# The output projection of a transformer layer as seven products of half-size blocks, on one NeuronCore of Trainium2

## The chip, the cores and the metric

The kernel runs on one core of a Trainium2 chip. The core has five engines that run side by side: TensorE (PE in the profile; its weight loads are shown as PEld), VectorE (DVE), ScalarE (ACT), GpSimd (POOL) and SyncE (SP), which here only starts transfers. SBUF is the on-chip memory of 128 partitions, PSUM the eight banks into which TensorE writes (one bank holds 128 x 512 float32). The metric is the device time of one execution in microseconds; lower is better.

## The reference

One decoder layer over 1024 tokens of width 1024, in float32 (DEPTH = 1, so alpha = 2^(1/4)):

```python
h = x @ w_in                      # columns: pool | q | k | v | forget gate
pool = pool_mixer(h[pool])        # 4 groups of 128 channels, trailing means over 2, 4, 8, 16 tokens minus
                                  # the token, then a 128 x 128 linear map and a scale per channel
attn = forgetting_attention(q, k, v, f)      # 8 heads of 64, causal, logit bias from cumulated log gates
x = layer_norm(alpha * x + concat(pool, attn) @ w_out)
x = layer_norm(alpha * x + square(relu(x @ w_mlp1)) @ w_mlp2)
```

`w_out` is 1024 x 1024: the output projection is a product of (tokens x mixture channels) with (mixture channels x output channels).

## The kernel before

**Precision.** Every float32 operand of a large product is split into a high part (rounded to the matmul's own format, `fp32r`) by ScalarE and a low part (the rest) by VectorE; `split` (line 70) makes both. A product then takes three matmuls, high x high, high x low and low x high (`three`, line 80).

**Buffers.** SBUF tiles come from five tags with a fixed number of buffers (line 48): S 3, U 2, B 14, Q 10, A 9. A B buffer holds 8 KB per partition, the others about 4. A tile gets a buffer when an earlier tile of its tag has been used for the last time; until then whatever writes it waits. PSUM banks are tags too: s 3, pt 2, pv 1, mm 2.

**Order.** The program is written out in Python, one instruction after the other; a planner, which knows the buffers and a cost for each operation, makes from it one fixed order per engine at build time. Within an engine, instructions run in that order, each behind its semaphores. `tc.issue_after(i)` puts the instructions traced in its block behind instruction i on i's engine.

**Stages.** (1) Values and gates of all tokens (lines 165 to 210); as this runs, blocks 3 to 7 of `w_out` are loaded, split and written to DRAM as high and low parts (`wo_dram`, lines 190 to 210). (2) The pooling groups 3, 2 and 1 (`pool_group`, line 264, 48 matmuls of 512 columns each) and the first key and query projection (`qk_proj(0)`). Each group's linear map (`pool_linear`) is 6 matmuls; its result goes to `mix_dram`. (3) Four pairs of heads, each in 8 units of 256 queries (loop at line 680): `att_probs` makes the probabilities, `att_values` transposes them and multiplies with V. Between the steps of a unit `fillstep` (line 669) takes pieces of other matmul work from a generator, at a rate that spreads it over the pair: in pairs 0 to 2 the next pair's projection, in the last pair `last_fill` (line 485): the projection of pooling group 0 in two halves, its linear map, the loads of the output weights and the output rows 0 and 1. Each output row is 2 halves x 8 blocks x 3 matmuls (`out_proj`, line 576), the mixture's transposed blocks being the weights (`mixes`) and `w_out`'s rows the moving operand. (4) After the pairs, rows 2 to 7 (loop at line 916): load x, the matmuls, then `normed` (line 592), which adds alpha x + product and norms the row on VectorE, and `x1_transposed` (line 736), which transposes a normed row with TensorE and makes the blocks that the MLP's products need. (5) The MLP, whose two products are already made as seven half-size products each (Winograd's form: A11, A12, A22, S1 to S4 on one side, B11, B21, B22, T1 to T4 on the other). Its first products, `first.p1` to `third.p2`, use A11 and A12 only (rows 0 to 3); `first.p6` is the first that needs S2, into which all rows go.

The attention results are stored unscaled in `mix_dram` and the reciprocal row sums in `rin_dram`; `attention_part` (line 548) loads both and multiplies.

## Time and profile before

| | us |
|---|---|
| median of 3 runs | 1033.78 |
| lowest, highest | 1032.7, 1034.51 |
| the profiled execution, its own time | 1033.61 |
| its span in the profile | 1031.8 |
| TensorE busy | 1015.8 |
| VectorE busy | 755.0 |
| ScalarE busy | 513.6 |
| GpSimd busy | 157.3 |

The profile is one execution. A matmul's recorded duration is longer than the time at which the next one can follow, since matmuls are pipelined; what a matmul costs is read from the distance of starts or from the chain that ended last, where it is shown as length of a run of matmuls. "Busy" leaves out waits and the instructions that only issue transfers. L12 is line 12 of the kernel.

### The profile page before, as it was taken

How to read it: one execution, taken by the hardware profiler on the slowest of the kernel's cores; microseconds unless marked ns; L12 is line 12 of the kernel's file. 1: busy time of each engine (PE TensorE's matmuls, PEld its weight loads, DVE VectorE, ACT ScalarE, POOL GpSimd, SP SyncE). 2: the span in 40 equal slices, each digit the busy share in tenths (PEclk: the TensorE clock that was granted, in tenths of full speed). 3: DMA queues.
4: the chain of work that ended last, by engine and by line, in shares of the span. 5: the costliest groups of instructions: out<-in, count | busy, mean ns of one | idle time of the engine just before them, and what ended most of it. 6: DMA issues, size and time to landing. Idle time of an engine off the chain costs nothing.

```text
span 1031.8 us, 14130 instructions
## 1 busy us (share of the span) xinstructions
PE 1015.8 (98%) x4976; PEld 845.6 (82%) x4976; DVE 755.0 (73%) x1303; ACT 513.6 (50%) x825; POOL 157.3 (15%) x269
## 2 busy tenths in 40 slices
PE   9999999999999999999999999999999999999996
PEld 9988888888787888788888888888888888888884
DVE  6576777777767897989878778888866575565547
ACT  5423666666655332677766666668521121121152
POOL 0200112111110032112122121120100000000057
PEclk9999999999999999999999999999999999999998
DMA  9703311111483632239666566665999888878753
GB/s 358 283 23 107 100 52 46 37 30 62 144 286 131 197 141 103 81 132 371 250 264 258 229 258 244 239 253 195 356 300 300 284 284 265 280 239 272 236 181 122
DMA packets 113463, 206.17 MB, mean 200 GB/s; under 512 B 9640, under 2 KB 77672, under 8 KB 113392
## 3 DMA queue, kind: packets, MB, share of 16 engines
q1 hardware_dynamic: 94240, 136.97, 40.3%
q0 software_dynamic: 18720, 67.64, 17.0%
q8 instruction: 39, 0.64, 0.3%
q10 hardware_dynamic: 432, 0.66, 0.2%
q14 instruction: 32, 0.26, 0.1%
HBM read 132.29 MB, written 72.94 MB: 199 GB/s over the span
## 4 chain that ended last, share of the span: by engine, by line
PE 57%; DVE 2%; issue 0%; ACT 0%; DVEq 0%
PE s L1109 17%; PE s L769 11%; PE pv L1109 9%; PE mm L769 7%; PE pt L769 7%; PE pv L769 4%; PE pt L1109 2%; PE mm L1109 2%; DVE B L71 0%; DVE bns L613 0%; DVE A L638 0%; DVE pt L635 0%; DVE pt L1126 0%; DVE A L843 0%; DVE pv L1126 0%
## 5 line engine op out<-in xcount | busy, mean ns | idle before, releaser
L71 ACT CAST B<-S 128x1024 fp32r<-128x1024 f32 (+1 forms) x78 | 67.6, 880 | 162.1 <-DMA S<-in_w_dram 95.2
L769 PE MATMUL s<-B,Q 128*128 128x512 f32 x492 | 116.4, 389 | 0.2 <-ACT B L71 0.2
L769 PEld LDWEIGHTS s<-B,Q 128*128 128x128 f32 x492 | 92.3, 188 | 19.8 <-ACT B L71 0.7
L71 DVE TENSOR_TENSOR B<-S,B 128x1024 fp32r<-128x1024 f32 (+1 forms) x78 | 78.1, 1008 | 36.4 <-ACT B L71 36.3
L1109 PE MATMUL s<-B,Q 128*128 128x512 f32 x402 | 98.5, 390 | 0.0
L1109 PEld LDWEIGHTS s<-B,Q 128*128 128x128 f32 x402 | 75.5, 188 | 16.4
L71 ACT CAST Q<-S 128x1024 fp32r<-128x1024 f32 (+2 forms) x54 | 55.6, 1030 | 55.5 <-PE s L769 17.0
L894 POOL DMA_DIRECT2D hid_dram<-A x90 | 48.1, 538 | 218.2 <-ACT A L891 171.5
L1109 PE MATMUL s<-B,A 128*128 128x512 f32 x321 | 80.0, 394 | 0.0
L769 PE MATMUL pt<-B,Q 128*128 128x512 f32 x312 | 74.5, 389 | 0.0
L71 DVE TENSOR_TENSOR Q<-S,Q 128x1024 fp32r<-128x1024 f32 (+2 forms) x54 | 65.5, 1212 | 12.3 <-ACT Q L71 12.2
L1109 PEld LDWEIGHTS s<-B,A 128*128 128x128 f32 x321 | 60.4, 188 | 13.8
L769 PE MATMUL mm<-B,Q 128*128 128x512 f32 x300 | 71.6, 389 | 0.0
L769 PEld LDWEIGHTS pt<-B,Q 128*128 128x128 f32 x312 | 58.5, 188 | 12.1
L769 PEld LDWEIGHTS mm<-B,Q 128*128 128x128 f32 x300 | 56.3, 188 | 11.7
L423 PEld LDWEIGHTS pv<-A,B 128*128 128x128 f32 x320 | 51.1, 188 | 17.6 <-ACT A L403 7.0
L382 ACT ACTIVATE A<-A,nm 128x1024 f32<-128x1024 f32 (+7 forms) x64 | 49.7, 777 | 31.5 <-DVE nm L380 31.0
L423 PE MATMUL pv<-A,B 128*128 128x256 f32 x320 | 61.2, 293 | 3.2 <-DVE A L404 1.5
L404 DVE TENSOR_TENSOR A<-pt,A 128x512 fp32r<-128x512 f32 (+1 forms) x80 | 49.9, 633 | 16.7 <-ACT A L403 16.0
L892 DVE TENSOR_TENSOR A<-A,A 128x1024 f32<-128x1024 f32 x45 | 53.6, 1219 | 0.0
L366 POOL TENSOR_TENSOR A<-A,maskb 128x128 f32<-128x128 f32 x48 | 23.6, 494 | 194.4 <-DVE nm L380 132.0
L403 ACT CAST A<-pt 128x512 fp32r<-128x512 f32 (+1 forms) x80 | 41.4, 542 | 21.9 <-PE pt L402 21.2
(432 smaller groups left out, 2320.0 us busy)
## 6 DMA issues: line engine op xcount, KB each, us to landing
hid_dram<-A POOLq DMA_DIRECT2D x105, 512.0 KB, 3.9
S<-in_w_dram SPq DMA_DIRECT2D x62, 512.0 KB
Q<-hid_dram SPq DMA_DIRECT2D x98, 256.0 KB
A<-hid_dram SPq DMA_DIRECT2D x82, 256.0 KB
S<-in_wuqk_dram SPq DMA_DIRECT2D x12, 512.0 KB
wo_dram<-Q POOLq DMA_DIRECT2D x10, 512.0 KB, 4.5
B<-wo_dram SPq DMA_DIRECT2D x10, 512.0 KB
Q<-hid_dram SPq DMA_DIRECT2D x39, 128.0 KB
```

The source lines that it names most:

```text
L71: return nc.scalar.copy(hi, src).ins, nc.vector.tensor_tensor(lo, src, hi.bitcast(F32), ALU.subtract).ins
L366: nc.gpsimd.tensor_tensor(nb[:, qs], nb[:, qs], maskb, ALU.add)
L382: nc.scalar.activation(pt[:, :nk], pt[:, :nk], AF.Exp, bias=nm, scale=-1.0, accum_out=rsum[h][:, i : i + 1])
L403: nc.scalar.copy(tt[:, 0, ev], tp[:, ev])
L404: fill["sub"] = nc.vector.tensor_tensor(tt[:, 1, ev], tp[:, ev], tt[:, 0, ev].bitcast(F32), ALU.subtract).ins
L423: nc.tensor.matmul(ov, V[j][:, h].rearrange("p s d -> p (s d)"), tt[:, s, a:b], start=(j == 0 and s == 0), stop=(j == 2 * m + 1 and s == 1),)
L769: nc.tensor.matmul(dst, b[x][:, k], A[a][y][:, k], start=first and k == 0 and i == 0, stop=k == H - 1 and i == 2, skip_group_check=not first,)
L892: nc.vector.tensor_tensor(x, x, hi.bitcast(F32), ALU.subtract)
L894: nc.gpsimd.dma_start(hid_dram[self.u, :, i, AT[name] : AT[name] + 2 * CH], part.rearrange("p q n t -> p (q n t)"))
L1109: nc.tensor.matmul(dst, h[:, p_], w[q_], start=first and u == self.us[0] and j == 0, stop=u == self.us[-1] and j == 2, skip_group_check=no ...
```

## The change

The output product Y = M W is taken as 2 x 2 blocks of 512: M's columns are the pooled half (4 blocks of 128 channels) and the attention half, its rows the first and last 512 tokens; W's rows and columns are split likewise. With M11 = pooled part of the later tokens (the order of the token halves is turned so that the pooled halves come first), Winograd's form needs seven products of (512 x 512) x (512 x 512) in place of eight: A11 x B11, S3 x T3, S2 x T2, S1 x T1, A22 x T4, A12 x B21, S4 x B22.

- **Weights.** All of `w_out` is loaded in front, in four pairs of blocks (k and k + 4). `output_sums` forms T1 to T4 with four subtractions on GpSimd per k, `split_output_weights` makes high and low parts of B11; B21, B22; T1, T2 and T3, T4 (ScalarE, and VectorE or GpSimd), and all go to `wo_dram` (7 versions x 2 parts). Two of the four k are done between the value products, two between the pooling groups.
- **Pooling groups.** All four (3, 2, 1, 0) run in front of the pairs as `pool_group`, and all their linear maps too. `late_group`, `late_linear` and the old `last_fill` go.
- **Fill.** In the last quarter of pair 2's fill (`third_fill`), B11 is loaded and A11 and the pooled differences are made (`pooled_differences`). The last pair's fill is three of the seven products, A11 x B11, S3 x T3 and S2 x T2, 12 bank results, each copied to SBUF (`kept`) by ScalarE and, for the third product, added into the other two on GpSimd. Each attention product is queued behind the last fill piece (before: for the first 8 pieces only).
- **Attention blocks.** `first_part` and `later_part` load, scale and combine attention results with the pooled ones to S2, A22, S1, A12 and S4, in steps after the units of the last pair, and for the last 256 tokens after the pairs.
- **Rows.** After the pairs, four products are left. A first loop over r makes S1 x T1 and A22 x T4 and finishes rows 0 to 3; a second makes A12 x B21 and S4 x B22 and finishes rows 4 to 7. Rows 0 to 5 are normed with ScalarE and GpSimd (`on_pool`), 6 and 7 on VectorE. Three rows (5, 6, 7) are transposed among the first MLP products (before: row 7 alone).

```diff
+    WEIGHTS = ("B11", "B21", "B22", "T1", "T2", "T3", "T4")
+    wo_dram = dr.tile([len(WEIGHTS), 2, P, NG, CH], F32, name="wo_dram")
...
+    def output_sums(k):
+        (b1, b2), sub = raw[k], nc.gpsimd.tensor_tensor
+        t12, t34 = slot("Q", [2, CH], F32), slot("Q", [2, CH], F32)
+        sub(t12[:, 0], b1[:, 1], b1[:, 0], ALU.subtract)
+        sub(t12[:, 1], b2[:, 1], t12[:, 0], ALU.subtract)
+        sub(t34[:, 0], b2[:, 1], b1[:, 1], ALU.subtract)
+        sub(t34[:, 1], b2[:, 0], t12[:, 1], ALU.subtract)
+        raw[k] = ((0, b1[:, 0:1]), (1, b2), (3, t12), (5, t34))
+
+    def split_output_weights(k, i, tag, eng):
+        n, src = raw[k][i]
+        w = src.shape[1]
+        hi = slot(tag, [w, CH])
+        nc.scalar.copy(hi, src)
+        eng.tensor_tensor(src, src, hi.bitcast(F32), ALU.subtract)
+        for j, part in enumerate((hi.bitcast(F32), src)):
+            nc.gpsimd.dma_start(wo_dram[n : n + w, j, :, k].rearrange("n p c -> p n c"), part)
...
+            n = 2 * (t - 4) + half
+            if n % 4 == 0:
+                output_sums(n // 4)
+            split_output_weights(n // 4, n % 4, "S", nc.vector)
...
-    for g in EARLY:
+    for n, g in enumerate(POOLS):
+        if n in (1, 2):
+            load_output_weights(n + 1)
         run(pool_group(g, None, "A"))
-        if g == EARLY[0]:
+        if n == 0:
             gate_sum(neglog)
+        else:
+            if n > 1:
+                pool_linear(POOLS[n - 2], "A")
+            if n < 3:
+                output_sums(n + 1)
+                for i in range(4):
+                    split_output_weights(n + 1, i, "A", nc.vector if i < 2 else nc.gpsimd)
...
-    pool_linear(EARLY[0], "A")
+    pool_linear(POOLS[2], "A")
     run(g0)
+    pool_linear(POOLS[3], "A")
...
+    def pooled_differences(c):
+        new, old = pooled_part(2 + c), pooled_part(c)
         if c == 0:
+            kept["S"] = slot("B", F32B, F32)
+        put("A11", c, new, "B")
+        nc.gpsimd.tensor_tensor(kept["S"][:, c], new, old, ALU.subtract)
...
+    def block_product(dst, name, weight, r):
+        (hi, lo), w = mixes[name, r // 2], wo[weight]
+        ts_ = slice(r % 2 * P, (r % 2 + 1) * P)
+        for k in range(NG):
+            yield three(dst, (hi[:, k, ts_], lo[:, k, ts_]), (w[0][:, k], w[1][:, k]), k == 0, k == NG - 1)
+
+    def third_fill():
+        for n, _ in enumerate(qk_proj(NPAIR - 1, "mm")):
+            yield
+            if n == 23:
+                output_weights("B11")
+                for c in range(2):
+                    pooled_differences(c)
+
+    def last_fill():
+        output_weights("T3")
+        for c in range(2):
+            put("S3", c, kept["S"][:, c], "Q")
+        for n, (name, weight) in enumerate((("A11", "B11"), ("S3", "T3"), ("S2", "T2"))):
+            kept[n] = slot("B", [NT // 2, CH], F32)
+            for r in range(NT // 2):
+                dst = bank("mm")
+                yield from block_product(dst, name, weight, r)
+                nc.scalar.copy(kept[n][:, r], dst)
+                if n == 2:
+                    nc.gpsimd.tensor_tensor(kept[2][:, r], kept[2][:, r], kept[0][:, r], ALU.add)
+                    nc.gpsimd.tensor_tensor(kept[1][:, r], kept[1][:, r], kept[2][:, r], ALU.add)
+                if n == 0 and r == NT // 2 - 1:
+                    output_weights("T2")
...
+    def normed(t, xt):
         nm = Norm(xt, *gb, x1_dram[t])
-        for i, c in enumerate(nm.cols):
-            nc.vector.scalar_tensor_tensor(xt[:, c], xt[:, c], ALPHA, yp[i], ALU.mult, ALU.add)
-            nm.stats(i)
-        nm.on_vector(nc.gpsimd)
+        if t < NT - 2:
+            nm.on_pool()
+        else:
+            for i in range(2):
+                nm.stats(i)
+            nm.on_vector(nc.gpsimd)
...
+    load_rows()
+    output_weights("T1", "T4")
...
+    for r in range(4):
+        a, b = row(r), row(4 + r)
+        a0, a1, b0, b1_ = (y_[:, c] for y_ in (a, b) for c in both)
+        for half in (a0, a1):
+            stt(half, half, ALPHA, kept[1][:, r], ALU.mult, ALU.add)
+        p5, p4 = bank(), bank()
+        run(block_product(p5, "S1", "T1", r))
+        into(a1, a1, p5, ALU.add)
+        stt(b1_, b1_, ALPHA, p5, ALU.mult, ALU.add)
+        run(block_product(p4, "A22", "T4", r))
+        into(a0, a0, p4, ALU.add)
+        nc.gpsimd.tensor_tensor(b1_, b1_, kept[2][:, r], ALU.add)
+        stt(b0, b0, ALPHA, pre[:, r], ALU.mult, ALU.add)
+        normed(r, a)
+        if r == 0:
+            step(3, 1)
+        if r == 1:
+            step(3, 2)
+            output_weights("B21", "B22")
+        if r == 3:
+            x1_transposed(*done.pop(0))
+    for r in range(4):
...
+        b0, b1_ = (x[4 + r][:, c] for c in both)
+        p2, p3 = bank(), bank()
+        run(block_product(p2, "A12", "B21", r))
+        into(b0, b0, p2, ALU.add)
+        run(block_product(p3, "S4", "B22", r))
+        into(b1_, b1_, p3, ALU.add)
+        normed(4 + r, x[4 + r])
+        x1_transposed(*done.pop(0))
...
     first.p1()
     first.p2()
     first.split_t2()
+    x1_transposed(*done.pop(0), ("mm", "pv"))
     second.p1()
-
-    block("S2", lambda j: R1[j][:, 0], 3)
+    x1_transposed(*done.pop(0), ("mm", "pv"))
     second.sums()
     second.split_t2()
+    block("S2", lambda j: R1[j][:, 0], 3)
     x1_transposed(*done.pop(0))
```

More of the change, by code (lines that the diff above doesn't have):

```diff
@@ new lines, in trunk, with output_weights, put @@
+    mixes, wo, done, gb = {}, {}, [], []
+    F32B = [2, NG, 256]
+    def output_weights(*names):
+        for name in names:
+            wo[name] = slot("B", [NG, CH]), slot("B", [NG, CH])
+            for i, part in enumerate(wo[name]):
+                nc.sync.dma_start(part.bitcast(F32), wo_dram[WEIGHTS.index(name), i])
+    def put(name, c, src, tag):
+        if tag == "B":
+            both = slot("B", F32B)
+            mixes[name, c] = hi, lo = both[:, 0], both[:, 1]
+        else:
+            mixes[name, c] = hi, lo = slot(tag, [NG, 256]), slot(tag, [NG, 256])
+        split(hi, lo, src)
@@ new lines, in pooled_part, with attention_part @@
+    def pooled_part(m):
+        mf = slot("S", [NG, 256], F32)
+        nc.sync.dma_start(mf, mix_dram[m, :, 0:NG, :])
+        return mf
+    def attention_part(m):
+        mf, rb = slot("S", [NPAIR, 256], F32), slot("S", [NPAIR, 256], F32)
+        nc.sync.dma_start(mf, mix_dram[m, :, NG : 2 * NG, :])
+        for e in range(2):
+            rows = rin_dram[e::2, m * 256 : (m + 1) * 256].rearrange("(o p) t -> o p t", o=1)
+            nc.sync.dma_start(rb[e * HD : (e + 1) * HD], rows.to_broadcast([HD, NPAIR, 256]))
+        return mf, rb
@@ L584, in trunk, with two, later_part, one @@
-    gb = []
+                nc.gpsimd.tensor_tensor(kept["S"][:, c], mf, kept["S"][:, c], ALU.subtract)
+                put("S2", c, kept["S"][:, c], "Q")
+        def two():
+            with tc.issue_after(fill["sub"]):
+                nc.gpsimd.tensor_tensor(old, mf, old, ALU.add)
+                put("A22", c, mf, "B")
+                put("S1", c, old, "B")
+        return one, two
+    def later_part(c):
+        mf, rb = attention_part(2 + c)
+        def one():
+            with tc.issue_after(fill["sub"]):
+                nc.vector.tensor_tensor(mf, mf, rb, ALU.mult)
+                nc.gpsimd.tensor_tensor(kept["S"][:, c], mf, kept["S"][:, c], ALU.subtract)
+                put("A12", c, mf, "Q")
+        def two():
+            with tc.issue_after(fill["sub"]):
+                put("S4", c, kept["S"][:, c], "Q")
+        return one, two
@@ L673, in fillstep @@
             piece = next(fill["gen"], None)
-            if piece and fill["pieces"] < 8:
-                fill["piece"], fill["pieces"] = piece, fill["pieces"] + 1
+            if piece:
+                fill["piece"] = piece
     order = [(p, e, m) for p in range(NPAIR - 1) for e in range(2) for m in (3, 2, 1, 0)]
@@ L679, in trunk, with step @@
     pend = None
+    parts = {}
+    def step(m, i):
+        if m < 0:
+            return
+        if i == 0:
+            parts[m] = first_part(m) if m < 2 else later_part(m - 2)
+        else:
+            parts[m][i - 1]()
     for n, unit in enumerate(order):
@@ new lines, in trunk, with row @@
+    output_weights("T1", "T4")
+    pre, x, both = kept[0], [None] * NT, (slice(0, CH), slice(CH, D))
+    stt, into = nc.vector.scalar_tensor_tensor, nc.vector.tensor_tensor
+    rr[0] = 0
+    def row(t):
+        x[t] = slot("A", [D], F32)
+        nc.sync.dma_start(x[t], xn[t])
+        return x[t]
+    for r in range(4):
[19 more added lines that the diff above has]
+            x1_transposed(*done.pop(0))
@@ new lines, in trunk @@
+    for r in range(4):
+        if r == 3:
+            for un in units[:2]:
+                un.load_f()
+                un.split_f("Q" if un.u else "B")
+                if un.u == 0:
+                    un.load_g()
+                    un.sums(nc.gpsimd)
+        b0, b1_ = (x[4 + r][:, c] for c in both)
[6 more added lines that the diff above has]
+        x1_transposed(*done.pop(0))
```

185 lines of the change are left out of this document (28 added, 157 removed).

## The prediction

> **What bounds the kernel now.** I read the page's busy times first, then busy time by stage, then the chain that ended last.
>
> ```profile
> span 1031.8 us, 14130 instructions
> PE 1015.8 (98%) x4976; PEld 845.6 (82%) x4976; DVE 755.0 (73%) x1303; ACT 513.6 (50%) x825; POOL 157.3 (15%) x269
> ```
>
> TensorE is busy 98% of the span. That is an average, so the next view gives the busy time of each engine stage by stage (columns: the stretch, its length, then PE, weight loads, DVE, ACT, POOL, each with its count, granted clock, DMA share, GB/s).
>
> ```profile
> 50.00:109.00 59.00, 59.00 (x273) 48.92 (x272) 38.62 (x78) 17.39 (x28) 0.76 (x1) 1.00 0.19 66
> 109.00:267.00 158.00, 156.16 (x909) 130.22 (x908) 116.42 (x288) 101.81 (x220) 30.08 (x74) 1.00 0.18 56
> 267.00:338.00 71.00, 68.15 (x385) 55.08 (x385) 51.79 (x125) 42.23 (x90) 7.48 (x15) 1.00 0.58 194
> 338.00:406.00 68.00, 68.00 (x327) 56.78 (x326) 56.58 (x97) 18.85 (x33) 16.32 (x18) 1.00 0.46 155
> 406.00:424.70 18.70, 18.46 (x90) 14.82 (x88) 18.31 (x32) 12.07 (x21) 2.93 (x4) 1.00 0.17 61
> ```
>
> The stretches are the pooling groups with the first projection, pairs 0 to 2, the last pair, the output projection of rows 2 to 7, and the first MLP products up to the first that needs row 7. PE idles only 2.85 us in the last pair, 1.84 in the pairs before, and nowhere in the output projection. So matmuls taken away are worth their full time if nothing new stalls PE. The fifth row warns: there VectorE is busy 18.31 of 18.70 us. The chain says the same (start, length, work):
>
> ```profile
> 415.57 1.20 DVE B L71 x2
> ...
> 423.38 0.61 DVE Q L758
> 424.00 0.02 issue
> 424.02 0.63 ACT B L71
> 424.65 0.04 issue
> 424.69 8.50 PE s L769 x36
> 433.19 2.72 PE pt L769 x12
> ```
>
> Up to 424.69 the chain runs through VectorE, making block S2 of the MLP's operand out of row 7; from there it is PE. PE loses only 0.24 us there, but VectorE has nothing to give. The last row gives the price of a matmul of 512 columns: 2.72 / 12 = 0.2267 us.
>
> **The change part by part.** **Matmuls.** The output product had 8 row tiles x 2 halves x 8 blocks x 3 = 384 matmuls; seven products of 4 row tiles x 4 blocks x 3 make 336. Ahead of the pairs 54 are added (48 of group 0's projection, 6 of its linear map; +12.2 us), the fill of the last pair goes from 150 to 144 (-1.4), and what follows the pairs from 288 to 192 (-21.8). Together 48 fewer: **-10.9 us**. Transposes, attention and MLP products are the same.
>
> **Last pair.** Group 0's projection, its two linear maps and the output rows 0 and 1 leave the fill, and with them the waits of their loads. Of the 2.85 us that PE idles there I count 1.0 as gone; bounds -2.8 (all gone) and 0, since new waits (A11 and S2 from DRAM) can take their place: **-1.0 us**.
>
> **Where the tail begins.** Today all output weights are in SBUF before the pairs end. In the change the fourth product needs T1 (hi and lo, 1 MB each) in two of the 14 buffers of tag B. Counting buffers through the last pair: V holds 4, T2 2, the kept products 3, A22 and S1 2 each, the difference S 1: 14, all taken. T1 gets buffers only when T2's last fill matmul or V's first tiles are done, and the gain and shift rows of the norm are in front of it. The fill ends two steps before the last attention product, since each attention product is now queued behind its fill piece. The nearest rows for these two steps are the last ones of today's last pair (PE, in order of time):
>
> ```profile
> 333.48 0.49 PE L402 MATMUL pt<-ident,A 128*128 128x128 f32 x3
> 333.72 0.73 PE L423 MATMUL pv<-A,B 128*128 128x256 f32 x4
> 334.54 0.50 PE L423 MATMUL pv<-A,B 128*128 128x256 f32 x2
> 335.80 0.40 PE L423 MATMUL pv<-A,B 128*128 128x256 f32 x2
> ```
>
> They last 2.7 us. For the load, the DMA view (KB, us from issue to landing) and one stretch of today's weight loads:
>
> ```profile
> x_dram<-A POOLq DMA_DIRECT2D x12, 256.0 KB, 2.6
> out_dram<-Q POOLq DMA_DIRECT2D x4, 512.0 KB, 3.2
> 298.00:300.00 2.00, 2.00 (x16) 1.82 (x15) 2.00 (x7) 1.29 (x2) 0.00 (x0) 1.00 1.04 408
> ```
>
> 256 KB more cost 0.6 us, so 2.0 is fixed, and 2 MB land 2.0 + 8 x 0.6 = 6.8 us after issue. 6.8 - 2.7 = 4.1 us of idle PE; the rows of gain and shift (1 MB, 2.5 us at 408 GB/s) start some 1.5 us earlier and push a little. I take **+4.5 us**, bounds 2 (V's first tile serves T1 early) and 7 (all of the rows' 2.5 us ahead of it). While it waits, VectorE and POOL work off what is ready.
>
> **The tail's other engines.** Rows 0 to 5 are now normed by ScalarE and POOL, and POOL adds more. What an add costs, and what POOL and VectorE do to each other (POOL's four sums of the first MLP unit, the norm passes and splits of VectorE with POOL active and without, the POOL norm's groups at the kernel's end, transposes):
>
> ```profile
> 365.19 1.29 POOL L817 TENSOR_TENSOR S<-S,S 128x512 f32<-128x512 f32 x1 [7.11 <-DVE B L71]
> 366.56 1.62 POOL L818 TENSOR_TENSOR U<-S,S 128x512 f32<-128x512 f32 x1
> 368.14 1.74 POOL L820 TENSOR_TENSOR S<-S 128x512 f32<-128x512 f32 x1
> 369.84 2.28 POOL L819 TENSOR_TENSOR S<-U,S 128x512 f32<-128x512 f32 x1
> 363.89 1.21 DVE L71 TENSOR_TENSOR B<-S,B 128x1024 fp32r<-128x1024 f32 x1
> 365.33 3.40 DVE L635 SCALAR_TENSOR_TENSOR A<-A,mv,B 128x512 f32<-128x512 f32 x2
> 368.73 2.23 DVE L71 TENSOR_TENSOR Q<-S,Q 128x1024 fp32r<-128x1024 f32 x1
> 376.52 1.40 DVE L635 SCALAR_TENSOR_TENSOR A<-A,mv,B 128x512 f32<-128x512 f32 x2
> L652 POOL TENSOR_TENSOR Q<-Q,S 128x1024 f32<-128x1024 f32 x4 | 9.6, 2411 | 265.4 <-ACT Q L651 265.4
> L646 ACT ACTIVATE U<-Q,rt 128x1024 bf16<-128x1024 f32 x4 | 4.6, 1149 | 0.1
> L651 ACT ACTIVATE Q<-Q,rt 128x1024 f32<-128x1024 f32 x4 | 5.0, 1240 | 3.0 <-DVE rt L650 3.0
> 405.88 0.60 PE L742 MATMUL pv<-ident,A 128*128 128x128 f32 x4
> 406.31 0.60 PE L742 MATMUL mm<-ident,A 128*128 128x128 f32 x4
> 406.67 2.98 PE L769 MATMUL s<-B,B 128*128 128x512 f32 x12
> ```
>
> The two scale passes took 3.40 us against 1.40, the split 2.23 against 1.21: VectorE lost 3.0 us, and POOL's four adds 6.93 - 4 x 1.29 = 1.8, while they overlapped. Lost together 4.8 of 5.2 us: an operation of VectorE that reads two operands from SBUF runs in turn with a POOL add, not beside it. So I sum both as one resource, from the pairs' end to the first product that needs row 7. POOL: 4 adds of 512 columns for the lower rows, 6 norms of 2 x 2.41, unit 0's four sums, some 3 adds of transposed rows: 11 x 1.29 + 28.9 = 43 us. VectorE with two SBUF operands: 12 scaled adds of a half row (0.7 each, half an L635 pair), four passes of 1.21 on the last operands, 8 scale passes of rows 6 and 7, two unit splits, some 15 half passes for transposed rows, T2, S2 and unit sums: 35 x 0.7 + 6 x 1.21 = 32. Together 75 us. PE in that stretch: 192 x 0.2267 = 43.5, eight rows of transposes at 0.79 (405.88 to 406.67), six products of 2.72: 66 us. 9 us too much, of which the 4.5 us at the front and the head start of adds on products already made absorb the larger part. I take **+2.7 us**, bounds 0 (unit sums and splits done early, as POOL's rows at 365 show today, 40 us ahead of their use) and 9.
>
> **Pooling groups and weights.** Group 0 joins the stage at 50 to 109, with the weights' sums and splits. VectorE's 38.62 us there grow by group 0 (4 passes of 1.21) and six splits for two of the four k (3.8 us); POOL adds per k four sums and two splits, 4 x 1.29 + 2 x 2.41 = 10, 20 us for two k, all in turn with VectorE in the worst case: 67 us, in a stage that grows to 59 + 12.2 = 71. It fits, with little left; PE has eight banks and the next group's weights ahead of it. The weight parts go out by POOL's DMA queue and are 14.7 MB, written and read, against 5.2; at 408 GB/s the added writes are 23 us of a queue that this stage uses at 0.19. I take **+1.0 us**, bounds 0 and 5 (a group's weights late by one 1.21 pass and one POOL split, at two group changes).
>
> Sum: -10.9 - 1.0 + 4.5 + 2.7 + 1.0 = -3.7 us. The profiled execution took 1033.61 us (1.81 outside its span), 0.17 below the median of 1033.78, so 1029.9 there and **1030** for the median.
>
> **The rivals.** *All is hidden:* loads and adds find room, and only the matmuls and part of the last pair's idle time count, -10.9 - 0.5: 1022. For it: PE runs through equally crowded stages without a gap today. Against it: the count of B buffers, which leaves T1 no place earlier.
>
> *DMA eats it, no net change:* behind T1 queue T4 (2 MB), row vectors (1), eight rows of x (4), the last attention part (1), B21 and B22 (4): 14 MB with T1, 35 us at 408 GB/s. PE wants B22 about 4.5 + 21.8 + 2.7 + 0.8 = 30 us after the pairs, 32.5 after the fill. Late by 2.5 to 3, if x rows don't come in before: 1033. Against it: T4 may wait behind row 1's T1 product, and four to eight buffers of tag A fall free as attention ends, so x can come early.
>
> *Slower, the tail set by POOL and VectorE in turn:* the first norm reaches POOL only after 5.4 us of PE plus about 5 us of ScalarE and VectorE (two passes of 1.1, one of 1.24, small ones). From there some 66 of the 75 us remain, ending at 10.9 + 66 = 77 against PE's 66: +11 in place of +2.7, in total +4.6: 1038. It decides for a loss once the tail costs more than 10.9 + 1.0 - 4.5 - 1.0 = 6.4 us. For it: the 4.8 of 5.2 us above, and VectorE's 18.31 of 18.70. Against it: adds that read PSUM need not share.
> [...]
>
> **How the numbers follow.** Forecast 0.32, all hidden 0.13, DMA 0.22, POOL and VectorE in turn 0.33. 0.2%, 2.1 us, is about what a measurement of this kernel tells from no change: faster 0.45 (the first two), same 0.22, slower 0.33. The forecast's own range is 1026 to 1031.5. All bounds at their best give 1022, at their worst 1044; I keep 1023 to 1040 for 8 in 10.
>
> **What would show it.** PE matmuls fall from 4976 to 4928. Right for the front: the first product with T1 waits 2 to 7 us for a DMA from the weights in DRAM, after the last attention product. Right for the tail: POOL nearly full between the pairs' end and the first product with S2, VectorE's two-operand passes stretched, PE waiting a few us for a transposed row or S2. Right for the groups: PE without gaps of over 1 us before pair 0. Wrong if T1 is there in time, if waits for B21 or B22 show, or if a product in the last pair's fill holds up attention by several us.

## The result, and the profile after

The changed kernel takes 1098.41 us (median of four runs, 1095.05 to 1099.71) against 1033.49 of the kernel before on the same chip: a ratio of 1.0623, interval 1.0596 to 1.0649. It is 6% slower, where 1030 was forecast and 1040 was the top of the range. The profiled execution took 1097.66, its span is 64.1 us longer than before. The page of the changed kernel (busy times and, in 40 slices, the granted TensorE clock in tenths):

```profile
span 1095.9 us, 14175 instructions
...
PE 1030.9 (94%) x4928; PEld 851.6 (78%) x4928; DVE 788.8 (72%) x1293; ACT 548.6 (50%) x876; POOL 267.0 (24%) x330
...
PEclk9989989999999887989999999999999999999998
```

The 48 matmuls are gone, as forecast (4928 against 4976), and yet TensorE is busy 15.1 us longer and idle 65.0 us in place of 16.0. With 10.9 us fewer to do, that is 26 us of slower matmuls and 49 us of new idle time: 26 + 49 - 10.9 = 64. The slices show the first part. In the kernel before every slice was at 0.9 of full speed or more (mean 0.997), and now the mean is 0.967; behind the wait for group 3's weights it is 0.50 (57.00 to 61.00), the half clock of the text below:

```profile
PEclk9999999999999999999999999999999999999998
```

TensorE's instructions of the changed kernel in order of time say where it was lost (start, length, work, and in brackets the idle time ahead and what ended it):

```profile
137.71 0.77 PE L401 MATMUL s<-Q,Q 128*128 128x512 f32 x1 [4.59 <-DVE Q L369]
...
374.94 0.97 PE L449 MATMUL pv<-A,B 128*128 128x256 f32 x6 [0.23 <-DVE A L430]
...
415.07 1.11 PE L758 MATMUL s<-ident,A 128*128 128x128 f32 x4 [7.09 <-POOL A L652]
...
484.88 8.49 PE L785 MATMUL s<-B,Q 128*128 128x512 f32 x36
```

And the same place in the kernel before, beside the last attention product (335.80) and the first MLP product with S2 (424.69) shown in the prediction:

```profile
108.31 1.07 PE L375 MATMUL s<-Q,Q 128*128 128x512 f32 x4
```

The first attention score, the end of the last attention product and the first MLP product with S2, which needs every normed row, cut the span in four. (The row at 415.07 is the first transpose of a normed row.) "Expected" is the kernel before with the matmuls added or removed by the prediction's count and nothing else:

| stretch | before | expected | after | lost |
|---|---|---|---|---|
| to the first score | 108.3 | 120.5 | 137.7 | 17.2 |
| the pairs | 227.9 | 226.5 | 238.2 | 11.7 |
| tail, to the first product with S2 | 88.5 | 66.7 | 109.0 | 42.3 |
| the rest | 607.1 | 607.1 | 611.0 | 3.9 |

What TensorE waited for, in the view of waits (total us, times, longest):

```profile
PE s L758 <- POOL A L652: 11.1, 3, 7.1
PE s L83 <- DMA B<-wo_dram: 5.6, 1, 5.6
PE s L82 <- ACT B L71: 4.8, 1, 4.8
PE pv L449 <- DVE A L430: 4.7, 7, 1.6
PE s L401 <- DVE Q L369: 4.6, 1, 4.6
PE pv L449 <- ACT A L429: 3.7, 3, 2.9
PE mm L82 <- DVE A L952: 3.7, 1, 3.7
PE s L758 <- DVE A L637: 3.4, 1, 3.4
```

Each of the first three stretches has waits of its own. Only the second is the one that was forecast, T1's load. The first is GpSimd's last pass of a norm, the third the weights of pooling group 3, the fifth the query casts of pair 0.

### The profile page after: what moved, and what is told of

The parts are those of the page before. It is cut to its first block, busy times and chain, and to the rows that moved or that the text cites. A ratio compares the mean times of both kernels' runs of the same rounds, so it can differ in the third digit from the quotient of the medians.

```text
span 1095.9 us, 14175 instructions
## 1 busy us (share of the span) xinstructions
PE 1030.9 (94%) x4928; PEld 851.6 (78%) x4928; DVE 788.8 (72%) x1293; ACT 548.6 (50%) x876; POOL 267.0 (24%) x330
## 4 chain that ended last, share of the span: by engine, by line
PE 66%; issue 9%; DVE 7%; POOL 4%; ACT 4%; DMA 1%; SPq 0%; DVEq 0%; POOLq 0%; ACTq 0%
PE s L1154 16%; PE pv L1154 8%; PE s L785 7%; PE mm L785 6%; PE pt L785 6%; PE pv L785 3%; PE pv L449 3%; PE mm L84 2%; PE mm L82 2%; PE mm L83 2%; PE s L401 2%; PE pt L1154 2%; PE mm L1154 2%; PE pt L428 2%; DVE Q L366 1%
## 5 line engine op out<-in xcount | busy, mean ns | idle before, releaser
L71 ACT CAST B<-S 128x1024 fp32r<-128x1024 f32 (+1 forms) x81 | 70.8, 886 | 174.7 <-DMA S<-in_w_dram 84.7
L71 DVE TENSOR_TENSOR B<-S,B 128x1024 fp32r<-128x1024 f32 (+1 forms) x81 | 86.7, 1078 | 47.5 <-ACT B L71 47.5
L71 ACT CAST Q<-S 128x1024 fp32r<-128x1024 f32 x47 | 49.4, 1052 | 60.1 <-PE s L785 18.0
L651 POOL TENSOR_TENSOR Q<-Q,S 128x1024 f32<-128x1024 f32 x4 | 9.7, 2420 | 264.9 <-ACT Q L650 264.8
L449 PEld LDWEIGHTS pv<-A,B 128*128 128x128 f32 x320 | 51.0, 188 | 25.6 <-ACT A L429 11.2
L71 DVE TENSOR_TENSOR Q<-S,Q 128x1024 fp32r<-128x1024 f32 x47 | 60.5, 1287 | 13.4 <-ACT Q L71 13.4
L785 PEld LDWEIGHTS mm<-B,Q 128*128 128x128 f32 x300 | 56.3, 188 | 11.7
L430 DVE TENSOR_TENSOR A<-pt,A 128x512 fp32r<-128x512 f32 (+1 forms) x80 | 49.7, 634 | 21.1 <-ACT A L429 20.1
L82 PE MATMUL mm<-B,B 128*128 128x512 f32 x152 | 62.9, 414 | 0.0
L83 PE MATMUL mm<-B,B 128*128 128x512 f32 x152 | 61.3, 403 | 0.0
```

Of the source, the lines that this page charges most:

```text
L71: return nc.scalar.copy(hi, src).ins, nc.vector.tensor_tensor(lo, src, hi.bitcast(F32), ALU.subtract).ins
L82: nc.tensor.matmul(dst, a[0], b[0], start=first, stop=False)
L83: nc.tensor.matmul(dst, a[0], b[1], start=False, stop=False)
L430: fill["sub"] = nc.vector.tensor_tensor(tt[:, 1, ev], tp[:, ev], tt[:, 0, ev].bitcast(F32), ALU.subtract).ins
L449: nc.tensor.matmul(ov, V[j][:, h].rearrange("p s d -> p (s d)"), tt[:, s, a:b], start=(j == 0 and s == 0), stop=(j == 2 * m + 1 and s == 1),)
L785: nc.tensor.matmul(dst, b[x][:, k], A[a][y][:, k], start=first and k == 0 and i == 0, stop=k == H - 1 and i == 2, skip_group_check=not first,)
```

## The experiments

The times below stand beside 1098.4 of the changed kernel. Ratios are to the kernel before, which took 1032.3 to 1032.9 beside these runs; the changed kernel was not timed again beside them. Stretches are read from one trace each. Four kernels below that change only what lies behind the pairs have pairs of 235.6 to 241.5 us, against 238.2 of the changed kernel, so a difference of some 3 us in one stretch says nothing by itself.

**Is the half clock a cause or a companion?** First, waits by hand in the kernel before, at the fifth product of four late steps:

```diff
     def p5(self):
         self.k2 = bank("pv")
+        if self.s in STALL:        # {6: 3, 8: 10, 10: 18, 12: 30}
+            g = y[(self.s - 1) % 4 + 4][:, 0:P]
+            nc.gpsimd.tensor_tensor(maskb, g, g, ALU.subtract)
+            for _ in range(STALL[self.s]):
+                nc.gpsimd.memset(maskb, 0.0)
+            nc.tensor.matmul(self.k2[:, 0:P], identb, maskb, start=True, stop=True)
```

> The kernel before, with four artificial waits of TensorE in the second MLP product (steps 6, 8, 10 and 12): ahead of the fifth product of the step one small matmul reads a tile that GpSimd rewrites 3, 10, 18 and 30 times (a memset of 128x128 took 0.20 us) after the end of the product before it. By these numbers and about 0.9 us for the add that starts each chain, the waits are about 1.5, 2.9, 4.5 and 6.9 us, 15.8 in all. Theory (a wait costs more than itself, since the granted clock falls to a half after it and stays there for some us): matmuls of 512 columns take about 0.45 us in place of 0.2267 behind the two longer waits, for 3 to 7 us each, so the time is 3 to 7 us more than the sum of the waits: +19 to +23. Rival (the half clock in the changed kernel has another cause, such as the load of all engines or the DMA): the matmuls behind the waits stay at 0.2267 us and the time grows by the sum of the waits, 16 us, or less where VectorE's later work hides part.

It took 1054.88, ratio 1.0214 (1.0192 to 1.0236). Its rows in order of time, each wait followed by the 12 matmuls of 512 columns behind it:

```profile
795.52 0.26 PE L1163 MATMUL pv<-maskb,identb 128*128 128x128 bf16 x1 [5.67 <-POOL maskb L1162]
795.54 5.21 PE L1110 MATMUL pv<-B,Q 128*128 128x512 f32 x12
...
801.52 2.91 PE L1110 MATMUL s<-B,Q 128*128 128x512 f32 x12
...
840.84 0.22 PE L1163 MATMUL pv<-maskb,identb 128*128 128x128 bf16 x1 [2.92 <-POOL maskb L1162]
840.87 4.59 PE L1110 MATMUL pv<-B,Q 128*128 128x512 f32 x12
...
885.85 0.27 PE L1163 MATMUL pv<-maskb,identb 128*128 128x128 bf16 x1 [2.76 <-POOL maskb L1162]
885.87 4.49 PE L1110 MATMUL pv<-B,A 128*128 128x512 f32 x12
...
931.21 0.22 PE L1163 MATMUL pv<-maskb,identb 128*128 128x128 bf16 x1 [1.99 <-POOL maskb L1162]
931.23 3.04 PE L1110 MATMUL pv<-B,A 128*128 128x512 f32 x12
```

The waits came out at 13.3 us in all, not 15.8 as intended, and the longest stands behind the shortest chain of GpSimd (3 writes), the shortest behind the longest (30). Twelve such matmuls take 2.91 us at full speed (801.52). Behind the wait of 1.99 us they take 3.04, behind 2.76 and 2.92 they take 4.49 and 4.59, behind 5.67 they take 5.21; the granted clock there is 1.00, 0.63, 0.62 and 0.53. TensorE's busy time is 6.8 us up on the kernel before (1022.6 against 1015.8), nearly all of it in slower matmuls. The time grew by 22.0 us, as the theory had it. So idling alone brings the half clock, whatever GpSimd does ahead of it: here a wait of 2.76 us was enough and one of 1.99 was not. In this kernel, where TensorE is the bound, the wait of 2.76 us cost 4.3 (2.76 + 4.49 - 2.91).

Then the reverse: unused matmuls in the changed kernel's waits, to keep the array busy.

```diff
+    def warm(dst, n):
+        four = identb.rearrange("p (o q) -> p o q", o=1).to_broadcast([P, 4, P])
+        for _ in range(n):
+            nc.tensor.matmul(dst.rearrange("p (o q) -> p o q", o=4), identb, four, start=True, stop=True)
...
         p5, p4 = bank(), bank()
+        if r == 0:
+            warm(p5, 26)           # and 21, 20, 30, 14, 14, 15 in six other places
```

> The changed kernel, with bf16 matmuls of 512 columns that nothing uses put where TensorE waits (21 ahead of group 3's projection, 20 ahead of the first attention scores, 26 ahead of the first T1 product, 30, 14 and 14 ahead of the transposes of rows 0, 2 and 6, 15 ahead of the first product with B21), each about as long as the wait in its place, into the bank that the real work overwrites. Theory (the half clock comes from idling): the granted clock stays at 1.0 behind those places; of the 26 us that TensorE's busy time grew by (1030.9 + 10.9 - 1015.8) the larger part goes, and of it what was on the path: 3.4 us in front of the pools, 5 us at the first attention scores, 2 us behind T1, and little in the tail, where GpSimd and VectorE set the end anyway: 8 to 20 us less than the changed kernel, 1078 to 1090. Rival (the clock falls for another cause): the clock falls at the same places, and the time is the same or longer, 1098 to 1103.

It took 1098.07, ratio 1.0638 (1.0618 to 1.0657): no change. The page and the groups of this kernel (the added matmuls are those from identb):

```profile
PE 1050.2 (96%) x5068; PEld 856.5 (78%) x5068; DVE 798.0 (73%) x1293; ACT 549.4 (50%) x876; POOL 267.0 (24%) x330
```

```profile
L100 PE MATMUL s<-identb 128*128 128x512 bf16 x126 | 28.4, 381 | 0.5 <-ACT A L325 0.5
L100 PE MATMUL mm<-identb 128*128 128x512 bf16 x14 | 3.2, 380 | 0.0
```

Without the 31.6 us of added matmuls TensorE's own work is 1018.6 us, 12.3 less than in the changed kernel: about half of the slow clock is gone. The time that it does not work rose by the same 12.4 us (1096.0 - 1018.6 = 77.4 against 65.0). The clock theory falls here, and so does the rival's reason, since the clock did stay up in six of the seven places (granted clock 1.00 behind them; behind the first scores it fell again, after a wait of 2.05 us): in these stretches other engines set the time, and a faster TensorE only waits longer. The part of the half clock that went was a companion of the loss, not its cause; the other half was not tested.

**The front.** Group 3's weights ahead of the output weights:

```diff
+    first_w = slot("S", [KT, P], F32)
+    nc.sync.dma_start(first_w, wuqk[POOLS[0]])
     for k in range(2):
         load_output_weights(k)
...
-        w = load_w(wuqk[g])
+        w = load_w(wuqk[g], first_w if g == POOLS[0] else None)
```

> The changed kernel, with only the load of pooling group 3's projection weights moved ahead of the output weights' loads and splits, into a buffer of tag S of its own (two are left for the splits' high parts). Theory (the wait of 4.80 us before group 3 comes from the three S buffers, held by the splits until their high parts have landed in DRAM, so that these weights are loaded at 47.9 us in place of 18): the wait and the half clock behind it go, 4.8 + 3.4 = 8 us less than the changed kernel, 1090; the first attention scores start at 129 to 131 us in place of 137.7. Rival (the DMA queues themselves are full from 45 to 60 us, share 0.98 to 1.00): the wait moves to the next weights and under 3 us are gained, 1095 to 1098.

1090.52, ratio 1.0553 (1.0527 to 1.0578): 7.9 us, as the theory had it; the first score starts at 130.16. The waits of SyncE's queue in the changed kernel, and the load as it ran (SyncE in order of time), show what was undone:

```profile
SPq L75 <- DMA wo_dram<-S: 33.6, 2, 31.6
```

```profile
47.91 10.79 SPq L75 DMA_DIRECT2D S<-in_wuqk_dram  x3
```

The queue stood 31.6 us until a split's high part had left its S buffer. SyncE in the kernel before issued the same loads 30 us earlier:

```profile
18.07 2.94 SPq L75 DMA_DIRECT2D S<-in_wuqk_dram  x3
```

The preparation left out:

```diff
-        sub(t12[:, 0], b1[:, 1], b1[:, 0], ALU.subtract)   # and three more
-        raw[k] = ((0, b1[:, 0:1]), (1, b2), (3, t12), (5, t34))
+        raw[k] = ((0, b1[:, 0:1]), (1, b2), (3, b1), (5, b2))
...
-        nc.scalar.copy(hi, src)
-        eng.tensor_tensor(src, src, hi.bitcast(F32), ALU.subtract)
-        for j, part in enumerate((hi.bitcast(F32), src)):
+        for j, part in enumerate((src, src)):
```

> The changed kernel with the preparation of the output weights left out: no sums and no splits of them on GpSimd, ScalarE and VectorE, the loaded blocks are written to DRAM as they are (as both parts, the same number of writes and bytes), so the product is made with other weights; everything behind it is unchanged. Theory (the preparation on GpSimd and VectorE in turn, and the S buffers that it holds, cost the whole 17.2 us by which pair 0 starts later than 108.3 + 12.2): the first attention scores start at 120.5 to 123 us in place of 137.7, and the time falls by 15 to 17, to 1081 to 1084. Rival (the fourth group's own passes, and DMA traffic of 14.7 MB in this stage, cost a good part): the scores start at 126 us or later, and the time stays above 1087.

1077.66, ratio 1.0433 (1.0415 to 1.0450): 20.7 us, more than expected. The first score starts at 123.22, 2.7 us behind the count of matmuls, so the fourth group itself is nearly free: the preparation costs the rest, with the same writes to DRAM.

Half of it on VectorE:

```diff
-        (b1, b2), sub = raw[k], nc.gpsimd.tensor_tensor
+        (b1, b2), sub = raw[k], (nc.gpsimd if k < 2 else nc.vector).tensor_tensor
...
-                    split_output_weights(n + 1, i, "A", nc.vector if i < 2 else nc.gpsimd)
+                    split_output_weights(n + 1, i, "A", nc.vector)
```

> The changed kernel, with the preparation of the second half of the output weights (eight sums, four of the eight splits) on VectorE in place of GpSimd. GpSimd loses 8 x 1.29 + 4 x 2.41 = 20 us between 76 and 128 us, VectorE gains 8 x 0.69 + 4 x 1.22 = 10.4 us by its own durations. Theory (the two take turns, so that GpSimd's 20 us are VectorE's too, and VectorE is late with the casts ahead of the first attention scores): scores start 5 to 9 us earlier, at 129 to 133 us, and the time falls to 1088 to 1093. Rival (VectorE is late by its own amount of work): the scores start at 138 us or later, and the time is 1098 to 1105.

1086.04, ratio 1.0517 (1.0499 to 1.0534): 12.4 us, more than the theory's range. 5.9 of them are in front of the first score (131.81); the pairs end 10.4 us earlier. More work on the late engine made it earlier. VectorE and GpSimd of the changed kernel, in order of time, show how that can be:

```profile
102.68 3.87 DVE L71 TENSOR_TENSOR B<-S,B 128x1024 fp32r<-128x1024 f32 x1
106.48 5.28 DVE L294 TENSOR_TENSOR Q<-Q 128x1022 f32<-128x1022 f32 x1
```

```profile
103.07 2.40 POOL L212 TENSOR_TENSOR Q<-Q,A 128x1024 f32<-128x1024 f32 x1
...
106.87 1.31 POOL L201 TENSOR_TENSOR Q<-Q 128x512 f32<-128x512 f32 x1
108.13 1.29 POOL L203 TENSOR_TENSOR Q<-Q,Q 128x512 f32<-128x512 f32 x1
109.39 1.28 POOL L202 TENSOR_TENSOR Q<-Q,Q 128x512 f32<-128x512 f32 x1
```

GpSimd's adds keep their 1.3 and 2.4 us. VectorE's pass (1.22 us by itself, at 73.66) ends at 111.8, 1.1 us behind the third of the adds (110.7): it waited out all three. It is not always VectorE that waits: three of GpSimd's adds between 78.97 and 89.18 took 2.2 to 3.2 us.

**The last pair.** The eight sums of operand blocks on VectorE:

```diff
-                nc.gpsimd.tensor_tensor(kept["S"][:, c], mf, kept["S"][:, c], ALU.subtract)
+                nc.vector.tensor_tensor(kept["S"][:, c], mf, kept["S"][:, c], ALU.subtract)
...             # the same for the pooled differences, S1 and S4
```

> The changed kernel, with the eight sums and differences of the operand blocks in pairs 2 and 3 (pooled differences, S2, S1, S4) on VectorE in place of GpSimd. Theory (in the last pair ScalarE's and VectorE's queues stand behind a GpSimd add of 2.4 us, as the cast for S1 that waited 4.28 us for it, and VectorE's splits of 1.22 us take 2.4 to 3.3 beside it; attention's casts queue behind them): the last attention product ends 4 to 8 us earlier than at 375.3 and the time falls to 1090 to 1094. Rival (what attention stands behind are the loads of the row factors and the amount of VectorE's work, not GpSimd): the last attention product ends within 2 us of 375.3, and the time is 1096 to 1101.

1088.63, ratio 1.0542 (1.0526 to 1.0558): 9.8 us. The last attention product ends at 368.5, 7.4 us earlier, and the pairs take 230.7 us, outside the spread named above. This theory holds.

**The tail, one cause at a time.** T1 first:

```diff
-    load_rows()
-    output_weights("T1", "T4")
+    output_weights("T1")
+    load_rows()
+    output_weights("T4")
```

> The changed kernel, with T1 loaded ahead of the norm's gain and shift rows (1 MB) in the tail. Theory (the wait of 5.63 us for T1 is on the path): the wait becomes 3 to 4.5 us, the half clock behind it shortens, and the time falls by 2 to 4, to 1094 to 1096. Rival (the tail's end is set by all its loads together, or by the norms): the first T1 product starts earlier, the transposes of row 0 wait longer, and the time stays within 1 us of 1098.

1095.45, ratio 1.0612 (1.0595 to 1.0629), 3.0 us below the changed kernel's median with intervals that overlap: not told apart from no gain. The wait did not go. It came in three, 2.5, 2.4 and 1.3 us for the parts of T1 and T4, 6.2 in place of 6.0.

Norms on VectorE:

```diff
-        if t < NT - 2:
-            nm.on_pool()
-        else:
-            for i in range(2):
-                nm.stats(i)
-            nm.on_vector(nc.gpsimd)
+        for i in range(2):
+            nm.stats(i)
+        nm.on_vector(nc.gpsimd)
```

> The changed kernel, with the norm of rows 0 to 5 in the tail taken back to VectorE, as rows 6 and 7 have it and as the kernel before had it for all rows; GpSimd loses 6 x 2 passes of 2.41 us. Theory (GpSimd's norm chain bounds the tail: it is 93 to 100% busy from 410 to 460 us, and TensorE waits 11.1 us for its last pass): those waits and the half clock behind them go, and the tail from the pairs' end to the first product with S2, 108.7 us, shortens by 10 to 25; time 1075 to 1088. Rival one (VectorE and GpSimd are one resource, and VectorE is already 10 of 10 us busy from 450 to 470): VectorE takes over as the bound, and the tail stays within 5 us, 1093 to 1103. Rival two (the DMA, at share 1.0 from 390 to 420 us, sets the tail): no change, 1096 to 1100, and TensorE waits for B21 or x rows.

1094.31, ratio 1.0593 (1.0569 to 1.0616). The tail is 6.2 us shorter (102.8 in place of 109.0), the pairs end 3.8 us later, and the intervals of the two times overlap; TensorE's longest wait is 6.4 us for one of VectorE's additions. That is nearest to rival one: VectorE takes GpSimd's place.

Rows of x ahead of B21 and B22:

```diff
-            output_weights("B21", "B22")      # at r == 1
...
+        if r == 3:
+            a, b = row(r), row(4 + r)
+            output_weights("B21", "B22")
```

> The changed kernel, with the four rows 2, 6, 3 and 7 of x (2 MB) loaded ahead of B21 and B22 (4 MB) in the tail. Theory (VectorE gets to row 2 at 422 us in place of about 408 since its row of x queues behind B21 and B22 with the DMA at share 1.0 from 390 to 420 us, and the norms of rows 2 to 5 are late with it): row 2's first pass starts before 412 us, the waits at 428.6 (3.66 us) and some of those behind it go, B21 comes up to 5 us later and makes a wait of 2 to 5 us instead; the time falls by 3 to 8, to 1090 to 1095. Rival (GpSimd's norms set the tail whenever the rows come): GpSimd stays full, and the time stays within 2 us of 1098.

1087.17, ratio 1.0536 (1.0514 to 1.0557): 11.2 us, more than expected, 8.0 of them in the tail. In the changed kernel SyncE issued them last:

```profile
389.68 8.85 SPq L485 DMA_DIRECT2D B<-wo_dram  x4
398.58 3.17 SPq L939 DMA_DIRECT2D A<-in_xn_dram  x4
```

VectorE reached row 2's first pass at 421.99 there, and at 404.56 with the rows first.

The last attention part behind row 0:

```diff
-        stt(b0, b0, ALPHA, pre[:, r], ALU.mult, ALU.add)
+        last = stt(b0, b0, ALPHA, pre[:, r], ALU.mult, ALU.add).ins
+        if r == 0:
+            fill["sub"] = last
```

> The changed kernel, with VectorE's product of the last attention part (the one that waits for the row factors' load until 391.6 us) put behind row 0's additions in VectorE's order. Theory (VectorE's queue stands 13.7 us behind that load, so row 0 gets to ScalarE's passes at 401.85 and to GpSimd at 410.25, and TensorE waits 7.09 us for its last pass): row 0's norm starts 4 to 8 us earlier, the wait for its transposes falls to 0 to 3 us, and the time falls by 3 to 7, to 1091 to 1095. Rival (rows 2 to 5 are late anyway, since their rows of x come at 421 us): the wait moves to the next rows, and the time stays within 2 us of 1098.

1098.23, ratio 1.0633 (1.0614 to 1.0652): no change, though neither side had the reason. VectorE in the changed kernel and then in this one:

```profile
391.63 1.22 DVE L543 TENSOR_TENSOR S<-S,S 128x1024 f32<-128x1024 f32 x1 [13.70 <-DMA S<-rin_dram]
```

```profile
394.97 1.29 DVE L946 SCALAR_TENSOR_TENSOR A<-A,B 128x512 f32<-128x512 f32 x2 [20.40 <-DMA A<-in_xn_dram]
```

With the wait for the row factors gone, VectorE stands 20.40 us for x of row 0; rows of x land 12 to 15 us after their issue (median 13.9 in the changed kernel), behind T1 and T4. Either way VectorE does next to nothing for the first 15 to 20 us of the tail.

**All together.** The six edits shown above (group 3's weights, half the preparation on VectorE, the parts, T1, x, row 0) in one kernel:

> The changed kernel with six edits together: group 3's weights early, the second half of the output weights' preparation on VectorE, the sums of the operand blocks in pairs 2 and 3 on VectorE, T1 ahead of the gain and shift rows, rows of x ahead of B21 and B22, and the last attention part behind row 0. Alone the ones measured gave 7.9, 9.8, 3.0 and 11.2 us; with 5 to 9 for the second and 3 to 7 for the last the sum is 40 to 48. Theory (the losses are separate waits in stages of their own): the time is 1050 to 1060. Rival (a common bound, the sum of GpSimd's and VectorE's work or the DMA, stands behind them, so that one wait takes another's place): 1065 or more.

1069.30, ratio 1.0355 (1.0340 to 1.0371): 29 us less, not the sum of 44.5 of the six alone. The first score starts at 125.35 and the pairs take 225.8 us, as expected; the tail is still 106.5 us (not 110.9, as an expectation below has it). The rival holds, and only for the tail. One wait that the six edits left is that for x of row 0, which is now issued behind T4 (SyncE, then VectorE):

```profile
357.59 3.86 SPq L488 DMA_DIRECT2D B<-wo_dram  x2
361.49 10.17 SPq L943 DMA_DIRECT2D A<-in_xn_dram  x8
```

```profile
372.69 1.29 DVE L954 SCALAR_TENSOR_TENSOR A<-A,B 128x512 f32<-128x512 f32 x2 [20.57 <-DMA A<-in_xn_dram]
```

VectorE's first pass of the tail starts 21.6 us behind the last attention product. With the norms of rows 0 and 1 on VectorE beside:

```diff
-        if t < NT - 2:
+        if 1 < t < NT - 2:
             nm.on_pool()
```

> The same six edits, and the norms of rows 0 and 1 on VectorE in place of GpSimd. Theory (the first transposes wait for GpSimd's chain, and early in the tail VectorE has room): 2 to 5 us less than with GpSimd's norms for these rows. Rival (VectorE is full there): the same or up to 4 us more.

1070.26, ratio 1.0367 (1.0347 to 1.0387): the same. So what bounds the tail was asked by leaving work out, on top of the six edits.

```diff
         def on_pool(self, rows=True):
...
-            nc.gpsimd.tensor_tensor(y, y, self.gam, ALU.mult)
-            nc.gpsimd.tensor_tensor(y, y, self.bet, ALU.add)
+            if rows:               # False for rows 0 to 5 of the tail
+                nc.gpsimd.tensor_tensor(y, y, self.gam, ALU.mult)
+                nc.gpsimd.tensor_tensor(y, y, self.bet, ALU.add)
```

> The kernel with the six edits undone (1069.3), with GpSimd's two passes of the norm, gain and shift, left out for rows 0 to 5 in the tail: 12 passes of about 2.5 us. Theory (GpSimd's passes, and VectorE in turn with them, bound the tail): the tail from the pairs' end to the first product with S2, 110.9 us, shortens by 15 to 25 and the time falls to 1045 to 1055. Rival (the loads bound it, share 1.0 for 40 us): it shortens by under 8, to 1062 or more, and TensorE waits for DMA instead.

1054.00, ratio 1.0208 (1.0192 to 1.0223): 15.3 us less, all of it in the tail, which is 91.2 us.

The norms on VectorE, with the edit of the tail shown above:

> The kernel with the six edits undone, with the norms of rows 0 to 5 on VectorE. Theory (GpSimd and VectorE are one resource in this stage): VectorE gains 6 x (2 statistics of 0.68 and 4 passes of 0.69) = 25 us, GpSimd loses 12 passes of 2.5 = 30 us, the sum hardly changes: 1064 to 1070. Rival one (GpSimd's chain alone bounds it): 1050 to 1058. Rival two (VectorE's amount alone bounds it, 78 us of work now, 103 then): 1080 or more.

1072.53, ratio 1.0388 (1.0370 to 1.0405): the tail takes 108.9 us against 106.5. Moving the norms, 30 us of GpSimd's passes against 25 of VectorE's, did not shorten it, while leaving GpSimd's passes out gave 15.3. Busy time from VectorE's first pass of the tail to the first product with S2, with the six edits, without GpSimd's passes, and with the norms on VectorE:

```profile
372.69:457.57 84.88, 62.96 (x274) 50.46 (x273) 72.95 (x121) 46.64 (x78) 53.06 (x33) 0.87 0.41 164
371.79:441.01 69.22, 60.95 (x274) 49.32 (x274) 63.29 (x123) 47.79 (x80) 21.81 (x22) 0.92 0.51 203
375.42:461.39 85.97, 65.58 (x275) 51.43 (x274) 85.10 (x160) 28.45 (x51) 27.52 (x28) 0.88 0.41 161
```

VectorE needs 73.0 us beside GpSimd's passes for work that takes 63.3 without them, 9.7 us more. With the norms its own it is full (85.1 of 86.0). How much of the 15.3 comes from the shorter chain of each row (two passes of GpSimd fall away) was not told apart.

Half of four weights' loads left out, the loaded half used twice:

```diff
+    HALF = ("T1", "T4", "B21", "B22")
...
+            n = 2 if name in HALF else NG
             for i, part in enumerate(wo[name]):
-                nc.sync.dma_start(part.bitcast(F32), wo_dram[WEIGHTS.index(name), i])
+                nc.sync.dma_start(part[:, :n].bitcast(F32), wo_dram[WEIGHTS.index(name), i, :, :n])
```

> The kernel with the six edits undone, with only the first half of T1, T4, B21 and B22 loaded (1 MB each in place of 2) and used twice: 4 of the 14 MB that this stage loads are left out, buffers and matmuls are the same. Theory (the loads only delay the stage's start): the wait for T1 goes and VectorE starts earlier, 3 to 8 us less, 1061 to 1066. Rival (the loads bound the whole stage): 4 MB at 408 GB/s, 10 us, and the half clock behind the waits: 10 to 16 us less, 1053 to 1059. If GpSimd and VectorE bound it alone: under 3 us less.

1063.54, ratio 1.0300 (1.0282 to 1.0317): 5.8 us, the range of a late start, not of a stage bound by its loads. VectorE's wait for x of row 0 falls from 20.57 to 16.57 us.

Both together:

> The kernel with the six edits undone, with GpSimd's gain and shift passes of rows 0 to 5 left out and the loads of T1, T4, B21 and B22 halved. If the two are separate bounds in a row, the gains add up (some 20 to 30 us less than 1069.3: 1040 to 1050), and the tail comes within 20 us of TensorE's own 66 us. If one alone bounds the stage, this is as fast as the better of the two alone, within 3 us.

1049.52, ratio 1.0167 (1.0152 to 1.0183): 19.8 us, against 15.3 + 5.8 = 21.1. The two are separate and add up. The tail is then 85.5 us, still 19 over the expected 66.7. VectorE stands 14.98 us of it for x of row 0, and is busy 64.5 of the 69.5 us behind that:

```profile
366.51 1.29 DVE L959 SCALAR_TENSOR_TENSOR A<-A,B 128x512 f32<-128x512 f32 x2 [14.98 <-DMA A<-in_xn_dram]
```

```profile
366.51:436.01 69.50, 60.25 (x273) 48.22 (x271) 64.54 (x123) 47.21 (x80) 22.26 (x22) 0.93 0.44 172
```

So the tail starts late and then VectorE is nearly full. No run loads x of row 0 ahead of T4; what that would give stays open.

## Why the prediction was wrong

**Matmuls (-10.9): right.** 4928, and the pairs of the kernel with six edits undone come out at their count (225.8 us, expected 226.5).

**T1 (+4.5, bounds 2 to 7): right in size, only half right in the reason.** TensorE waited 6.0 us for T1, 5.63 of them for its second half, just behind the last attention product. The prediction had both halves start at the end of the fill, once their buffers are free, and land after 6.8 us. The first half was issued at 370.31, 5.6 us ahead of the end of attention, and was only 0.40 late. The second stood in SyncE's queue behind the stores of the last attention result, as the chain that ended last shows:

```profile
377.50 0.44 DVE U L455
...
377.96 0.48 SPq L456
...
379.02 5.35 DMA B<-wo_dram
```

So the size is right in part by luck. Loading T1 ahead of the norm's rows only cut the wait in three.

**Pooling groups and weights (+1.0, bounds 0 and 5): wrong, 17.2.** "It fits, with little left" set 67 us of VectorE and GpSimd against a stage of 71. From 50.00 to 137.71 the two were busy 66.2 and 34.6 us, 100.7 in place of 67. And a sum below the length of a stage says nothing of when its last piece is done: VectorE's casts for pair 0 stood in its queue behind passes stretched to 3.9 and 5.3 us. The bound left out as well that the splits' high parts take the S buffers into which the next projection weights are loaded. "The next group's weights ahead of it" was true of the kernel before, not of the change. Two edits at the front gave 7.9 and 12.4 us, leaving the preparation out 20.7.

**Last pair (-1.0, bounds -2.8 and 0): wrong, +11.7 over the pairs.** Here the step counted loads alone as new waits, and put no price on what takes the place of the old fill: the sums and splits of A22, S1, S2, A12 and S4, which stand in ScalarE's and VectorE's queues between attention's own casts. Putting only their adds on VectorE gave 9.8 us. (Of the 11.7, some 3 us are within the spread of single traces.)

**The tail's other engines (+2.7, bounds 0 and 9): right mechanism, wrong size and wrong credit.** Of the 42.3 us lost in the tail the T1 wait is 6.0; some 36 remain, where the rival that had the two engines in turn gave 11. The failed sentence is "While it waits, VectorE and POOL work off what is ready". Busy time of the changed kernel in two stretches of the tail, the second up to TensorE's first product with S2:

```profile
376.40:391.60 15.20, 9.55 (x25) 6.86 (x26) 1.50 (x2) 0.19 (x1) 2.14 (x1) 0.57 0.77 188
391.60:485.10 93.50, 72.85 (x306) 58.86 (x305) 70.91 (x122) 48.69 (x81) 55.68 (x35) 0.85 0.45 178
```

In the first 15.2 us VectorE worked 1.50: nothing was ready, since row factors and x came behind the weights. From there VectorE and GpSimd were busy 70.9 and 55.7 of 93.5 us, 126.6 together, where 75 was summed. The 75 had durations without stretching, and left out the splits with one operand in PSUM and the norms' small operations. That adds which read PSUM need not share held here: up to 485.10 us, 17 of VectorE's passes of 128 x 512 with an operand in PSUM ran more than half of their time beside a pass of GpSimd, and took 0.67 to 0.69 us. The rival also gave the first norm "about 5 us of ScalarE and VectorE" on its way to GpSimd. ScalarE and then GpSimd of the changed kernel in order of time:

```profile
401.85 1.06 ACT L644 ACTIVATE U<-A 128x1024 bf16<-128x1024 f32 x1 [5.39 <-DVE A L949]
...
404.29 1.28 ACT L646 ACT_TABLE_LOAD   x1
...
406.62 1.06 ACT L644 ACTIVATE U<-A 128x1024 bf16<-128x1024 f32 x1 [0.73 <-DVE A L949]
...
408.95 1.23 ACT L650 ACTIVATE A<-A,rt 128x1024 f32<-128x1024 f32 x1
```

```profile
410.25 2.34 POOL L651 TENSOR_TENSOR A<-A,B 128x1024 f32<-128x1024 f32 x1 [1.28 <-ACT A L650]
```

It took 8.4 us, with a table load and row 1's passes (406.62) in between, and TensorE's queue stood behind this one row until 415.07. The rival had the first norm at GpSimd 10.9 us behind the pairs; it got there 34.3 us behind them (410.25). The rival was on the right side, but as one place with 11 us; the loss came in three stretches, and all the prediction's bounds at their worst gave 1044.

**DMA eats it (rival, 1033): half right.** It priced the late arrival of B22. What came late was x and the row factors, and moving x ahead of B21 and B22 gave 11.2 us alone; halving the weights gave 5.8 with the rest undone.

**The half clock was in no term.** It makes up 26 of the 75 us in TensorE's time, but with half of it gone the time stayed the same, so that half was not an extra price here.

## What to carry to other kernels

Moving matmul time to sums and splits cost more than it saved here, where VectorE and GpSimd had less room together than was summed (busy 100.7 us from 50.00 to 137.71 in place of 67, and the first score 17.2 us late). Such room has to be followed in the order of their queues: what is due first, what stands ahead of it, and which load holds the head of the queue. Before crediting an idle stretch to another engine, check that its operands have landed; a wait taken away from the head of a queue is worth only the distance to the next wait behind it (behind the row factors VectorE started at 391.63, and without that wait, behind x of row 0, at 394.97: 1098.41 and 1098.23 us). TensorE idle with a half clock behind it looks like two losses, and was one where another engine set the time (half of the slow clock gone, 1098.07 us).

## What the runs showed of the hardware

A wait of 1.99 us left the TensorE clock at full speed (12 matmuls in 3.04 us), one of 2.76 us brought it down (4.49 us, granted clock 0.63); in the kernel with the unused matmuls it fell in a wait of 2.05 us. A VectorE pass with both operands in SBUF waited out three GpSimd adds in a row, 5.28 us in place of 1.22, while the adds kept their 1.3 us. So handing 20 us of GpSimd's work to VectorE, the engine that was late, made the kernel 12.4 us faster.
